# One substitution for all 128 diagonal blocks, a decay difference computed on ScalarE, and an earlier place for the first chunk's preparation, in a hybrid DeltaNet and sparse-attention layer

## The chip, the cores and the metric

One NeuronCore of one Trainium2 chip runs the whole program. The metric is device time in microseconds (us) of that core; the kernel before takes 1951.12 us, the median of three runs (1950.59 to 1951.98).

## The reference, cut to what matters

A decoder layer over 1024 positions of 1024 channels: two token mixers side by side (A, a gated DeltaNet; B, sparse attention), an output projection, a convolutional FFN and a gated embedding. The change lies in mixer A, which has 4 heads of 128 channels:

```
qkv = silu(causal_dwconv(concat(q, k, v), conv_w))          # 4 taps a channel
q, k = l2norm(q) * dk ** -0.5, l2norm(k)
beta = sigmoid(b);  g = -exp(a_log) * softplus(a + dt_bias)
# in chunk_gated_delta_rule, for each chunk and head:
gcum  = cumsum(g)
lower = beta[..., None] * (k @ k.T) * exp(gcum_i - gcum_j)  # strictly below the diagonal
sol   = triangular_solve(lower + I, [beta * exp(gcum) * k, beta * v])
...                                                         # then a scan over the chunks
o = rmsnorm(o, norm_w) * silu(z)
```

Everything is float32. The kernel works in chunks of 128 positions, which gives 8 chunks x 4 heads = 32 triangular matrices of 128 x 128.

## The kernel before, in words

**Projections.** A float32 product is three matmuls on halves of the operands (`mm3`, L345 to L347). The input `u` lies transposed in SBUF as `uh` and `ul`. Weights come in column tiles of 128: a DMA on SP's queue loads `raw`, ScalarE (ACT) makes the high half `whi` (L324), GpSimd (POOL) the low half `wlo` (L313). A tile over all 1024 positions is 48 matmuls `pj`. First come 12 convolution tiles in the order k (4), q (4), v (4), each in one of two PSUM areas in turn (`psJ[n % 2]`), so that tile n+2 must wait until tile n's area has been read. Reading it is a chain: ACT copies with the fourth tap's weight into `y` (L521), VectorE (DVE) adds three taps, each reading PSUM (L524), ACT applies Silu (L525). `norms` squares a finished k or q tile on ACT and sums it by a matmul with ones, `pss` (L507). Then come 4 z tiles (`gate_tile`, L562: ACT evacuates each half of a tile, `yz`, from one of two PSUM buffers, and a DMA, `gates_d`, stores it). Tiles are counted here from 0: 0 to 11 are the convolutions, 12 to 15 z, 16 onwards other gates, which fill the scan over chunks.

**What the scan needs first.** `gdn_small` (from L805) makes beta, the cumulated decay `gc`, the norm factors `rk`, and writes rows of them to DRAM. `gdn_inverse32` makes for each chunk c the matrix L: load two rows over all partitions (`row4`), scale k (L931), the decay difference on DVE (L899, 4 instructions) and its exponential on ACT (L904), `pkk` on TensorE (PE), two DVE products (L935, L936), and a round trip through DRAM (`ld`, L937 and L941) which lays the 32 x 32 diagonal blocks, 4 for each matrix, out as one block a partition: 128 partitions in all. There 31 steps of forward substitution, two DVE instructions each (L954 into `tmp`, L956 into `blk`), invert the blocks. This is done in two halves: chunks 0 to 3 on partitions 0 to 63, then chunks 4 to 7 on partitions 64 to 127. Each half ends with a DMA `xd` (L959), a transposing copy (L960) and a second DMA `xd` (L961); behind the second half a memset clears `blk` (L962).

**Preparing a chunk.** `gdn_prep(0)`, from L965, loads the inverted blocks and the blocks of L off the diagonal back (L978, 8 DMAs; L981, 3 DMAs) and multiplies them up to the inverse of the 128 x 128 matrix: `pz`, `pt`, `pt1n` and so on, ten groups of small matmuls.

**What sets the order.** Generators run by hand say what is issued behind what: the inverse is advanced once per convolution tile. A tile scheduler puts instructions into each engine's queue by its own model of time, within `tc.issue_after` limits; each engine then takes its queue in order, and waits where an operand is not there. The calls around the change are:

```
            if inv:
                next(inv, None)
            run_all(cv)
        run_all(inv)
        ...
        for n in range(4):
            run_all(gate_tile(n))
        NG = 8
        self.gdn_prep(0)
```

## Time and profile before

| what | value |
|---|---|
| median of the three runs | 1951.12 us |
| the profiled execution's own time | 1951.64 us |
| its span, first to last instruction | 1949.9 us |
| PE busy | 1839.1 us, 94% |
| DVE / ACT / POOL busy | 63% / 47% / 36% |
| mean granted TensorE clock | 0.977 of full speed |
| the stretch of the change | about 60 to 285 us of the span |

The page gives busy time by engine and by slice; the timeline lists each instruction with its start, its length and, in square brackets, how long the engine had been idle before it and what ended that. PE matmuls overlap in their modelled lengths; the spacing of their starts is what counts. A granted clock of 1.00 is TensorE's level of 2.4 GHz, 0.50 that of 1.2 GHz.

### The profile page before, as it was taken

The numbers are of one execution on the slowest core, as the hardware profiler recorded it, in microseconds if no ns is written. First come the engines' busy times: TensorE is split into PE (matmuls) and PEld (weight loads), VectorE is DVE, ScalarE is ACT, GpSimd is POOL, SyncE is SP. The second block draws the span as 40 slices with busy tenths as digits, with TensorE's granted clock in tenths as the row PEclk, the third lists the DMA queues.
The fourth block names the chain that finished last, engine by engine and source line by source line (L and its number), as shares of the span: only waits on it lengthen the run. The fifth ranks groups of instructions, "written<-read, shape, count | busy, mean of one in ns | idle before, by whom it ended". The sixth has DMA issues, their size and how long they took to land.

```text
span 1949.9 us, 25814 instructions
## 1 busy us (share of the span) xinstructions
PE 1839.1 (94%) x9247; PEld 1528.1 (78%) x9247; DVE 1224.2 (63%) x2347; ACT 920.3 (47%) x1816; POOL 711.6 (36%) x537
## 2 busy tenths in 40 slices
PE   7999989999999999999889949999999999999998
PEld 7888778888888887778778837787787877777786
DVE  4448934432277667766694587777677764868643
ACT  4344223323276667766663334444454544446432
POOL 2132212223122112321162166666666664555200
PEclk9999989999999999999999969999999999999999
DMA  5133333333311010200073212232323257246201
GB/s 166 33 95 103 101 83 93 97 87 95 100 28 34 28 39 28 71 23 23 22 248 121 97 55 81 92 103 88 122 83 103 92 184 259 72 146 208 88 33 43
DMA packets 182622, 178.67 MB, mean 92 GB/s; under 512 B 27549, under 2 KB 133342, under 8 KB 182494
## 3 DMA queue, kind: packets, MB, share of 16 engines
q1 hardware_dynamic: 180272, 170.33, 27.8%
q10 hardware_dynamic: 2222, 6.69, 0.9%
q8 instruction: 73, 1.20, 0.3%
q14 instruction: 55, 0.45, 0.1%
HBM read 132.65 MB, written 44.34 MB: 91 GB/s over the span
## 4 chain that ended last, share of the span: by engine, by line
PE 34%; DVE 5%; POOL 4%; issue 3%; ACT 2%; DMA 2%; SPq 0%; POOLq 0%; ACTq 0%; DVEq 0%
PE q L345 3%; PE q L347 3%; PE q L346 3%; PE n L345 2%; PE n L347 2%; PE n L346 2%; PE pg L347 2%; PE pg L346 2%; PE pg L345 2%; PE pwo L347 1%; PE pwo L345 1%; PE pwo L346 1%; POOL whl L313 1%; POOL wdhl L313 1%; DMA araw<-acts 1%
## 5 line engine op out<-in xcount | busy, mean ns | idle before, releaser
L345 PE MATMUL pj<-uh,whi 128*128 128x512 f32 x640 | 260.0, 407 | 6.0 <-DVE y L524 3.7
L347 PE MATMUL pj<-uh,wlo 128*128 128x512 f32 x640 | 255.2, 399 | 0.0
L346 PE MATMUL pj<-ul,whi 128*128 128x512 f32 x640 | 255.2, 399 | 0.0
L313 POOL TENSOR_TENSOR wlo<-raw,whi 128x1024 fp32r<-128x1024 f32 x48 | 117.3, 2446 | 310.5 <-ACT whi L324 266.6
L313 POOL TENSOR_TENSOR whl<-s,whl 128x512 fp32r<-128x512 f32 x88 | 131.3, 1500 | 57.2 <-ACT whl L1344 57.2
L345 PEld LDWEIGHTS pj<-uh,whi 128*128 128x128 f32 x640 | 121.5, 190 | 33.3 <-ACT yz L562 2.8
L347 PEld LDWEIGHTS pj<-uh,wlo 128*128 128x128 f32 x640 | 121.3, 190 | 29.0
L346 PEld LDWEIGHTS pj<-ul,whi 128*128 128x128 f32 x640 | 121.8, 190 | 25.8
L313 POOL TENSOR_TENSOR whl<-raw,whl 128x512 fp32r<-128x512 f32 x66 | 105.8, 1605 | 58.1 <-ACT whl L1344 55.5
L313 POOL TENSOR_TENSOR wdhl<-wd,wdhl 128x512 fp32r<-128x512 f32 x66 | 98.9, 1507 | 76.1 <-ACT wdhl L1344 74.8
L313 DVE TENSOR_TENSOR whl<-araw,whl 128x512 fp32r<-128x512 f32 x77 | 84.4, 1103 | 56.5 <-ACT whl L1344 54.0
L1226 ACT ACTIVATE Pt<-Pt,nm 128x640 f32<-128x640 f32 (+7 forms) x128 | 93.0, 729 | 36.6 <-DVE nm L1224 36.2
L345 PE MATMUL q<-mxh,whl 128*128 128x512 f32 x264 | 103.8, 396 | 4.1 <-ACT u L106 2.8
L1256 DVE TENSOR_TENSOR Tl<-pt,Th 128x512 fp32r<-128x512 f32 (+1 forms) x152 | 92.4, 616 | 22.1 <-ACT Th L1255 17.9
L346 PE MATMUL q<-mxl,whl 128*128 128x512 f32 x264 | 103.5, 392 | 0.0
L347 PE MATMUL q<-mxh,whl 128*128 128x512 f32 x264 | 102.9, 392 | 0.2 <-POOL whl L313 0.2
L1255 ACT ACTIVATE Th<-pt 128x512 fp32r<-128x512 f32 (+1 forms) x152 | 78.5, 538 | 43.7 <-PE po L1259 33.7
L324 ACT ACTIVATE whi<-raw 128x1024 fp32r<-128x1024 f32 x48 | 50.5, 1052 | 82.8 <-PE pj L346 54.1
L1252 PE MATMUL pt<-ident,Pt 128*128 128x128 f32 x528 | 84.6, 280 | 5.0 <-DVE Tl L1256 3.2
L1294 POOL TENSOR_TENSOR tm<-tm 128x128 f32<-128x128 f32 x32 | 14.7, 459 | 197.2 <-DVE tm L1292 157.4
L126 DVE SCALAR_TENSOR_TENSOR yg<-c,cv,yg 128x511 f32<-128x511 f32 (+1 forms) x88 | 82.0, 936 | 1.0 <-ACT yg L123 0.9
L1344 ACT ACTIVATE whl<-s 128x512 fp32r<-128x512 f32 x88 | 54.7, 624 | 55.8 <-PE n L347 44.1
(533 smaller groups left out, 5181.8 us busy)
## 6 DMA issues: line engine op xcount, KB each, us to landing
raw<-in_w_up SPq DMA_DIRECT2D x44, 512.0 KB
raw<-in_w_in SPq DMA_DIRECT2D x40, 512.0 KB
araw<-acts SPq DMA_DIRECT2D x35, 512.0 KB
acts<-sd SPq DMA_DIRECT2D x44, 256.0 KB
gates_d<-yz SPq DMA_DIRECT2D x40, 256.0 KB
acts<-yv SPq DMA_DIRECT2D x33, 256.0 KB
gt<-gates_d SPq DMA_DIRECT2D x32, 256.0 KB
wd<-in_w_down SPq DMA_DIRECT2D x7, 1024.0 KB
```

The costliest lines, as they stand in the source:

```text
L126: self.body.nc.vector.scalar_tensor_tensor(y, src, w, y, ALU.mult, ALU.add)
L313: return eng.tensor_sub(lo, src, hi.bitcast(F32)).ins
L324: nc.scalar.activation(hi, raw, AF.Copy)
L345: nc.tensor.matmul(ps, lh, rh, start=start, stop=False, skip_group_check=more)
L346: nc.tensor.matmul(ps, lh, rl, start=False, stop=False, skip_group_check=more)
L347: nc.tensor.matmul(ps, ll, rh, start=False, stop=stop, skip_group_check=more)
L1226: nc.scalar.activation(Pt[:, hh, 0:nk], Pt[:, hh, 0:nk], AF.Exp, scale=2.0 ** -(h0 + hh + 1), bias=nm[:, br, hh:hh + 1], accum_out=rs[:, b ...
L1252: nc.tensor.transpose(pt[:, b, hh], Pt[:, hh, (b0 + b) * P:(b0 + b + 1) * P], self.ident)
L1255: nc.scalar.activation(Th[:, 0:m], pt[:, 0:m], AF.Copy)
L1256: nc.vector.tensor_sub(Tl[:, 0:m], pt[:, 0:m], Th[:, 0:m].bitcast(F32))
L1294: nc.gpsimd.tensor_add(tm[:, 0], tm[:, 0], tm[:, 1])
L1344: self.nc.scalar.activation(hi, src, AF.Copy)
```

## The change

1. The substitution runs once over 128 partitions, after all 8 chunks, and is cut into four shares by `yield` (behind steps 8, 15 and 22). L is made by 4 fused DVE instructions of 128 x 128 in place of 2 of 128 x 512. Each `xd` DMA is 512 KB, and there are 2 in place of 4.
2. For L, the difference with the cumulated decay is 4 Relu activations on ACT with a bias (`ngc`, the negated `gc`) in place of 4 DVE instructions.
3. Each share of the inverse is issued behind the last DVE tap of the convolution tile (`issue_after`); `gdn_small` is split in two, and its first part stands behind tile 1's taps. `a_log` and `dt_bias` are loaded by two DMAs on ACT's queue at the start.
4. `gdn_prep(0)` is issued behind the last matmul of z's second tile (tile 13), not after all four.

```diff
+                if t == 1:
+                    for i, name in enumerate(("a_log", "dt_bias")):
+                        nc.scalar.dma_start(self.adb[:, i * H:i * H + H], rows_to_all(io[name], H))
...
             for j in (2, 1, 0):
                 d = 3 - j
-                nc.vector.scalar_tensor_tensor(y[:, d:], ps[:, 0:SEQ - d], cwt(j), y[:, d:], ALU.mult, ALU.add)
-            nc.scalar.activation(qkvT[i], y, AF.Silu)
-
+                last["DVE"] = nc.vector.scalar_tensor_tensor(y[:, d:], ps[:, 0:SEQ - d], cwt(j), y[:, d:], ALU.mult,
+                                                             ALU.add).ins
+            last["ACT"] = nc.scalar.activation(qkvT[i], y, AF.Silu).ins
+
...
         order = [4, 5, 6, 7, 0, 1, 2, 3, 8, 9, 10, 11]
-        inv = None
+        inv = small = None
         for n, i in enumerate(order):
             cv = conv(n, i)
             next(cv)
             if n and order[n - 1] < 8:
                 norms(order[n - 1])
+            run_all(cv)
+            with self.behind(*last.values()):
+                if n == 1:
+                    self.gp = self.g1 = self.pool(ges, "gdn")
+                    small = self.gdn_small(pss)
+                    next(small)
             if order[n - 1] == 7:
+                run_all(small)
                 inv = self.gdn_inverse32()
             if inv:
-                next(inv, None)
-            run_all(cv)
-        run_all(inv)
+                with tc.issue_after(last["DVE"]):
+                    next(inv, None)
+        with tc.issue_after(last["DVE"]):
+            run_all(inv)
...
         for n in range(4):
             run_all(gate_tile(n))
+            if n == 1:
+                with tc.issue_after(self.mm_last):
+                    self.gdn_prep(0)
         NG = 8
-        self.gdn_prep(0)
...
-        al = t32("al", H)
-        nc.sync.dma_start(al, rows_to_all(io["a_log"], H))
-        db = t32("db", H)
-        nc.sync.dma_start(db, rows_to_all(io["dt_bias"], H))
+        al, db = self.adb[:, 0:H], self.adb[:, H:2 * H]
...
         nc.vector.tensor_copy(gc, ps[:, 0, 0:n])
+        ngc = self.ngc = k32("ngc")
+        nc.vector.tensor_scalar(ngc, ps[:, 0, 0:n], -1.0, None, ALU.mult)
...
-        rk = self.rsqrt(kss, "rk")
+        yield
+        rk = self.rsqrt(kss[0][:, 0, 0:NC * H], "rk")
...
         E = self.g1.tile([P, H, P], F32, name="E", tag="E", bufs=1)
         for h in range(H):
-            nc.vector.tensor_scalar(E[:, h], gr[:, h], self.gc[:, c * H + h:c * H + h + 1], 0.0, ALU.subtract,
-                                    ALU.min if causal else ALU.max)
+            j = slice(c * H + h, c * H + h + 1)
+            if causal:
+                nc.vector.tensor_scalar(E[:, h], gr[:, h], self.gc[:, j], 0.0, ALU.subtract, ALU.min)
+            else:
+                nc.scalar.activation(E[:, h], gr[:, h], AF.Relu, bias=self.ngc[:, j])
...
-        for hf in range(2):
-            for c in range(hf * NC // 2, (hf + 1) * NC // 2):
...
-                E = self.decay(c, gr, False)
-                pk = self.mm4(self.psgt("pkk"), k, k)
-                L = self.g1.tile([P, H, P], F32, name="L", tag="Z", bufs=2)
-                nc.vector.tensor_mul(L, pk, E)
-                nc.vector.tensor_mul(L, L, self.bc(self.beta[:, c * H:(c + 1) * H]))
...
-            m_ = hn * 4
-            pp = slice(hf * m_, hf * m_ + m_)
-            X_ = X[pp]
...
-            for j in range(31):
-                m, w = 31 - j, j + 1
-                t = tmp[pp, 0:m * w].rearrange("p (a b) -> p a b", b=w)
-                nc.vector.tensor_mul(t, Ls[pp, j + 1:, j].unsqueeze(2).to_broadcast([m_, m, w]),
-                                     X_[:, j, 0:w].unsqueeze(1).to_broadcast([m_, m, w]))
-                nc.vector.tensor_sub(X_[:, j + 1:, 0:w], X_[:, j + 1:, 0:w], t)
-                if j in (12, 20):
-                    yield
-            nc.sync.dma_start(self.xd[0, pp], X_)
-            nc.vector.tensor_copy(Ls[pp], X_.rearrange("p i j -> p j i"))
-            nc.sync.dma_start(self.xd[1, pp], Ls[pp])
+        X, Ls = X[:], Ls[:]
+        for c in range(NC):
...
+            E = self.decay(c, gr, False)
+            pk = self.mm4(self.psgt("pkk"), k, k)
+            L = self.g1.tile([P, H, P], F32, name="L", tag="Z", bufs=2)
+            for h in range(H):
+                j = c * H + h
+                nc.vector.scalar_tensor_tensor(L[:, h], pk[:, h], self.beta[:, j:j + 1], E[:, h], ALU.mult, ALU.mult)
+            nc.sync.dma_start(self.ld[c], L)
...
+        nc.vector.memset(X, 0.0)
+        nc.vector.memset(X.rearrange("p i j -> p (i j)")[:, 0:1024:33], 1.0)
+        for j in range(31):
+            m, w = 31 - j, j + 1
+            t = tmp[:, 0:m * w].rearrange("p (a b) -> p a b", b=w)
+            nc.vector.tensor_mul(t, Ls[:, j + 1:, j].unsqueeze(2).to_broadcast([P, m, w]),
+                                 X[:, j, 0:w].unsqueeze(1).to_broadcast([P, m, w]))
+            nc.vector.tensor_sub(X[:, j + 1:, 0:w], X[:, j + 1:, 0:w], t)
+            if j in (8, 15, 22):
+                yield
+        nc.sync.dma_start(self.xd[0], X)
+        nc.vector.tensor_copy(Ls, X.rearrange("p i j -> p j i"))
+        nc.sync.dma_start(self.xd[1], Ls)
         nc.vector.memset(blk, 0.0)
```

Where the program order of the engines moves, in three places.

DVE, around the taps of the last convolution tile (tile 11: the rows with `y<-pj`), in the kernel before:

```order
L960 COPY blk<-blk 64x1024
L956 TENSOR_TENSOR blk<-blk,tmp 64x22x10
L524 SCALAR_TENSOR_TENSOR y<-pj,cvw,y 128x1023
L954 TENSOR_TENSOR tmp<-blk 64x231
L524 SCALAR_TENSOR_TENSOR y<-pj,cvw,y 128x1022
L956 TENSOR_TENSOR blk<-blk,tmp 64x21x11
L524 SCALAR_TENSOR_TENSOR y<-pj,cvw,y 128x1021
L954 TENSOR_TENSOR tmp<-blk 64x240
```

and in the changed one, where a step's second instruction is L972:

```order
L972 TENSOR_TENSOR blk<-blk,tmp 128x10x22
L970 TENSOR_TENSOR tmp<-blk 128x207
L525 SCALAR_TENSOR_TENSOR y<-pj,cvw,y 128x1023
L972 TENSOR_TENSOR blk<-blk,tmp 128x9x23
L525 SCALAR_TENSOR_TENSOR y<-pj,cvw,y 128x1022
L525 SCALAR_TENSOR_TENSOR y<-pj,cvw,y 128x1021
L970 TENSOR_TENSOR tmp<-blk 128x192
```

Before, tile 11's taps stand in the second half at step 11; behind them come 20 more steps of that half. Now they stand in the only substitution at step 22; behind them come 8 more steps. The taps of tiles 9 and 10 stand at steps 7 and 15.

PE, behind the last projection matmul of z (tile 15) in the kernel before, where every group of the first chunk's preparation stands:

```order
L347 MATMUL pj<-uh,wlo 128x512
L912 MATMUL pz_2025<-blk 128x128 x4
L912 MATMUL pt_2032<-Z,blk 128x128 x4
L992 MATMUL pt1n<-ident,TT 128x128 x4
L912 MATMUL pqk<-qT,kT 128x128 x4
L912 MATMUL pz_2068<-TT,blk 128x128 x4
L1010 MATMUL pkt<-ident,kT 128x128 x4
L1015 MATMUL pvt<-ident,vT 128x128 x4
L912 MATMUL pt_2088<-Z,T_2038 128x128 x4
L912 MATMUL pz_2152<-blk 128x128 x4
L912 MATMUL pu<-vT,T_2087 128x128 x4
```

and in the changed one, where the first group stands behind 37 of tile 14's 48 matmuls:

```order
L345 MATMUL pj<-uh,whi 128x512
L930 MATMUL pz_1853<-blk 128x128 x4
L346 MATMUL pj<-ul,whi 128x512
L347 MATMUL pj<-uh,wlo 128x512
L345 MATMUL pj<-uh,whi 128x512
L346 MATMUL pj<-ul,whi 128x512
L347 MATMUL pj<-uh,wlo 128x512
```

The others follow between matmuls of tile 15 (`pt_1860` behind 11 of them, `pt1n` to `pkt` behind 34, `pvt` behind 40), and the last three stand where they all stood.

SP's queue, from the stores of the inverted blocks to the loads of the preparation, in the kernel before:

```order
L959 DMA xd<-blk 64x1024
L320 DMA raw<-in_w_in 128x8x128
L961 DMA xd<-blk 64x1024
L563 DMA gates_d<-yz 128x512
L978 DMA blk<-xd 32x4x32 x5
L563 DMA gates_d<-yz 128x512
L978 DMA blk<-xd 32x4x32 x3
L981 DMA blk<-ld 32x4x32 x2
L981 DMA blk<-ld 64x4x64
```

and in the changed one:

```order
L975 DMA xd<-blk 128x1024
L575 DMA gates_d<-yz 128x512
L977 DMA xd<-blk 128x1024
L320 DMA raw<-in_w_in 128x8x128
L575 DMA gates_d<-yz 128x512
L994 DMA blk<-xd 32x4x32 x8
L575 DMA gates_d<-yz 128x512
L997 DMA blk<-ld 32x4x32 x2
L997 DMA blk<-ld 64x4x64
```

The chain of store, memset and load is as it was, but with stores of 512 KB; the `gates_d` in it are those of tiles 12 and 13 now, and were those of tiles 14 and 15.

## Rows read from the trace of the kernel before

**Rows 1.** The page: the engines' busy time, its share of the span, and their instructions.

```profile
PE 1839.1 (94%) x9247; PEld 1528.1 (78%) x9247; DVE 1224.2 (63%) x2347; ACT 920.3 (47%) x1816; POOL 711.6 (36%) x537
```

**Rows 2.** PE's waits from 0 to 700 us, the longest that is not at the start: the line that waited and what ended the wait; us in total, times, longest.

```profile
PE pz L912 <- DMA blk<-ld: 4.5, 1, 4.5
```

**Rows 3.** Timelines of PE and ACT around the first two convolution tiles: start, length, engine, line, what, and in brackets the idle time before and what ended it.

```profile
72.73 0.47 PE L345 MATMUL pj<-uh,whi 128*128 128x512 f32 x1 [1.95 <-DVE y L524]
66.23 0.21 ACT L853 ACTIVATE small<-small 128x4 f32<-128x4 f32 x1 [1.93 <-DMA small<-in_a_log]
```

**Rows 4.** Timelines of PE, DVE and ACT from 203 to 241 us: the waits of tile 11 and of tile 13's first half, the last of tile 11's taps, the Silu behind it on ACT, and the start of tile 14.

```profile
203.23 0.47 PE L345 MATMUL pj<-uh,whi 128*128 128x512 f32 x1 [1.79 <-DVE y L524]
230.75 1.28 DVE L524 SCALAR_TENSOR_TENSOR y<-pj,cvw,y 128x1021 f32<-128x1021 f32 x1
232.12 1.06 ACT L525 ACTIVATE vT<-y 128x1024 f32<-128x1024 f32 x1 [9.67 <-DVE y L524]
234.66 0.50 PE L345 MATMUL pj<-uh,whi 128*128 128x512 f32 x1 [1.64 <-ACT yz L562]
240.37 0.40 PE L345 MATMUL pj<-uh,whi 128*128 128x512 f32 x1
```

**Rows 5.** Busy time by stretch: the stretch and its length, then PE, PEld, DVE, ACT and POOL (instructions), then the granted clock, the DMA share and GB/s.

```profile
170.00:255.00 85.00, 81.56 (x367) 66.05 (x366) 77.20 (x161) 29.04 (x34) 23.23 (x9) 0.98 0.31 82
204.60:207.90 3.30, 3.30 (x10) 2.56 (x9) 2.79 (x5) 2.37 (x3) 1.80 (x1) 0.50 0.24 84
255.00:260.00 5.00, 5.00 (x23) 4.00 (x23) 1.30 (x1) 0.60 (x1) 0.36 (x1) 1.00 0.58 194
266.00:276.20 10.20, 7.29 (x31) 6.73 (x32) 1.00 (x2) 1.19 (x2) 0.26 (x1) 0.50 0.54 147
```

**Rows 6.** Timelines of DVE, SP's queue and PE from the end of the substitution to the first matmul of tile 16; among them one line of ACT, which waited for the store issued at 262.81 (256 KB from 128 partitions).

```profile
251.96 1.14 DVE L960 COPY blk<-blk 64x1024 f32<-64x1024 f32 x1
253.12 0.85 SPq L961 DMA_DIRECT2D xd<-blk  x1
258.70 1.76 DVE L962 MEMSET blk<- 128x2048 f32 x1 [5.61 <-DMA xd<-blk]
260.50 2.22 SPq L978 DMA_DIRECT2D blk<-xd  x5
262.81 0.38 SPq L563 DMA_DIRECT2D gates_d<-yz  x1
264.96 0.60 ACT L562 ACTIVATE yz<-pj 128x512 f32<-128x512 f32 x1 [1.12 <-DMA gates_d<-yz]
262.54 0.40 PE L347 MATMUL pj<-uh,wlo 128*128 128x512 f32 x1
267.44 2.05 PE L912 MATMUL pz<-blk 128*128 128x128 f32 x8 [4.51 <-DMA blk<-ld]
279.56 1.13 PE L912 MATMUL pz<-blk 128*128 128x128 f32 x8 [0.74 <-DMA blk<-xd]
281.39 0.48 PE L345 MATMUL pj<-uh,whi 128*128 128x512 f32 x1
```

**Rows 7.** DVE's groups by line, 160 to 255 us: times, busy us, mean ns, idle before.

```profile
L956 DVE TENSOR_TENSOR blk<-blk,tmp 64x31 f32<-64x31 f32 (+15 forms) x62 | 27.2, 439 | 1.8
L954 DVE TENSOR_TENSOR tmp<-blk 64x31 f32<-64x31 f32 (+15 forms) x62 | 25.1, 404 | 2.5 <-DMA blk<-ld 0.4 <-issue 0.3
L524 DVE SCALAR_TENSOR_TENSOR y<-pj,cvw,y 128x1023 f32<-128x1023 f32 (+2 forms) x15 | 19.1, 1274 | 2.9 <-ACT y L521 2.7
L899 DVE TENSOR_SCALAR E<-row,gc 128x128 f32<-128x128 f32 x20 | 4.3, 271 | 0.0
```

**Rows 8.** Timelines of DVE and POOL: a memset at 64 us, and substitution steps beside the making of a low half.

```profile
64.03 0.91 DVE L949 MEMSET blk<- 64x1024 f32 x1 [0.15 <-DVE sg L491]
...
233.84 0.42 DVE L954 TENSOR_TENSOR tmp<-blk 64x252 f32<-64x252 f32 x1
234.29 2.58 DVE L956 TENSOR_TENSOR blk<-blk,tmp 64x252 f32<-64x252 f32 x1
234.20 2.39 POOL L313 TENSOR_TENSOR wlo<-raw,whi 128x1024 fp32r<-128x1024 f32 x1 [14.19 <-ACT whi L324]
```

**Rows 9.** Timelines of PE, SP's queue and DVE: the last k k products and q's sums, chunk 7's L on its way through DRAM, and the step that waited for it.

```profile
175.63 1.58 PE L912 MATMUL pkk<-kT 128*128 128x128 f32 x12
200.35 0.34 SPq L937 DMA_DIRECT2D ld<-L  x1
205.92 2.79 DVE L954 TENSOR_TENSOR tmp<-blk 64x31 f32<-64x31 f32 x2 [0.41 <-DMA blk<-ld]
```

**Rows 10.** ACT's groups by line, 130 to 180 us and 280 to 420 us, and one of DVE's, 280 to 420 us.

```profile
L904 ACT ACTIVATE E<-E 128x512 f32<-128x512 f32 x5 | 3.2, 632 | 13.9 <-DVE E L899 13.9
L904 ACT ACT_TABLE_LOAD x3 | 3.8, 1283 | 0.1
L1069 ACT ACTIVATE jk<-o 128x128 bf16<-128x128 f32 x24 | 7.1, 298 | 45.1 <-DVE o L1063 45.1
L1041 DVE SCALAR_TENSOR_TENSOR r<-pw,bg,vT 128x128 f32<-128x128 f32 x24 | 6.8, 344 | 0.1
```

**Rows 11.** Timeline of DVE around the first L.

```profile
139.07 1.88 DVE L931 TENSOR_TENSOR kT<-kT,row 128x512 f32<-128x512 f32 x1 [0.88 <-DMA row<-rows_d]
141.96 0.68 DVE L935 TENSOR_TENSOR L<-pkk,E 128x512 f32<-128x512 f32 x1
```

More of the change, by code (lines that the diff above doesn't have):

```diff
@@ L346, in mm3 @@
         nc.tensor.matmul(ps, lh, rl, start=False, stop=False, skip_group_check=more)
-        nc.tensor.matmul(ps, ll, rh, start=False, stop=stop, skip_group_check=more)
+        self.mm_last = nc.tensor.matmul(ps, ll, rh, start=False, stop=stop, skip_group_check=more).ins
     def rstd_of(self, ss, n, scale, name):
@@ L442, in mixers @@
         self.cvw = keep.tile([P, 81], F32, name="cvw")
+        self.adb = keep.tile([P, 2 * H], F32, name="adb")
         ges = ExitStack()
@@ L507, in norms @@
                 nc.tensor.matmul(pss[0][:, 0, j:j + 1], sq[:, c * P:(c + 1) * P], self.ones, start=True, stop=True)
-            if i == 7:
-                self.gp = self.g1 = self.pool(ges, "gdn")
-                self.gdn_small(pss[0][:, 0, 0:NC * H])
             if i == 3:
@@ L523, in conv @@
                 d = 3 - j
-                nc.vector.scalar_tensor_tensor(y[:, d:], ps[:, 0:SEQ - d], cwt(j), y[:, d:], ALU.mult, ALU.add)
-            nc.scalar.activation(qkvT[i], y, AF.Silu)
+                last["DVE"] = nc.vector.scalar_tensor_tensor(y[:, d:], ps[:, 0:SEQ - d], cwt(j), y[:, d:], ALU.mult,
+                                                             ALU.add).ins
+            last["ACT"] = nc.scalar.activation(qkvT[i], y, AF.Silu).ins
+        last = {}
         order = [4, 5, 6, 7, 0, 1, 2, 3, 8, 9, 10, 11]
-        inv = None
+        inv = small = None
         for n, i in enumerate(order):
@@ L915, in gdn_inverse32 @@
     def gdn_inverse32(self):
-        nc, gp, n, hn = self.nc, self.gp, NC * H, NC * H // 2
+        nc, gp, n = self.nc, self.gp, NC * H
         self.ld = self.dr.tile([NC, P, H, P], F32, name="ld")
@@ L925, in gdn_inverse32 @@
         tmp = gp.tile([P, 256], F32, name="tmp", tag="T1")
-        for hf in range(2):
-            for c in range(hf * NC // 2, (hf + 1) * NC // 2):
-                rk = self.row4(1, c, "qk", 2)
-                gr = self.row4(0, c, "gr", 2)
-                k = self.chunk(1, c)
-                nc.vector.tensor_mul(k, k, rk)
-                E = self.decay(c, gr, False)
-                pk = self.mm4(self.psgt("pkk"), k, k)
-                L = self.g1.tile([P, H, P], F32, name="L", tag="Z", bufs=2)
-                nc.vector.tensor_mul(L, pk, E)
-                nc.vector.tensor_mul(L, L, self.bc(self.beta[:, c * H:(c + 1) * H]))
-                nc.sync.dma_start(self.ld[c], L)
-                for h in range(H):
-                    p0 = (c * H + h) * 4
-                    l = self.ld
-                    nc.sync.dma_start(Ls[p0:p0 + 4], bass.AP(
-                        tensor=l.tensor, offset=l.offset + (c * P * H + h) * P,
-                        ap=[[32 * H * P + 32, 4], [H * P, 32], [1, 32]]))
-                if c % 2:
-                    yield
-            m_ = hn * 4
-            pp = slice(hf * m_, hf * m_ + m_)
-            X_ = X[pp]
-            nc.vector.memset(X_, 0.0)
-            nc.vector.memset(X_.rearrange("p i j -> p (i j)")[:, 0:1024:33], 1.0)
-            for j in range(31):
-                m, w = 31 - j, j + 1
-                t = tmp[pp, 0:m * w].rearrange("p (a b) -> p a b", b=w)
-                nc.vector.tensor_mul(t, Ls[pp, j + 1:, j].unsqueeze(2).to_broadcast([m_, m, w]),
-                                     X_[:, j, 0:w].unsqueeze(1).to_broadcast([m_, m, w]))
-                nc.vector.tensor_sub(X_[:, j + 1:, 0:w], X_[:, j + 1:, 0:w], t)
-                if j in (12, 20):
-                    yield
-            nc.sync.dma_start(self.xd[0, pp], X_)
-            nc.vector.tensor_copy(Ls[pp], X_.rearrange("p i j -> p j i"))
-            nc.sync.dma_start(self.xd[1, pp], Ls[pp])
@@ new lines, in gdn_inverse32 @@
+        X, Ls = X[:], Ls[:]
+        for c in range(NC):
+            rk = self.row4(1, c, "qk", 2)
+            gr = self.row4(0, c, "gr", 2)
+            k = self.chunk(1, c)
+            nc.vector.tensor_mul(k, k, rk)
+            E = self.decay(c, gr, False)
[5 more added lines that the diff above has]
+            nc.sync.dma_start(self.ld[c], L)
+            for h in range(H):
+                p0 = (c * H + h) * 4
+                l = self.ld
+                nc.sync.dma_start(Ls[p0:p0 + 4], bass.AP(
+                    tensor=l.tensor, offset=l.offset + (c * P * H + h) * P,
+                    ap=[[32 * H * P + 32, 4], [H * P, 32], [1, 32]]))
+            if c % 2:
+                yield
@@ new lines, in gdn_inverse32 @@
+        nc.vector.memset(X, 0.0)
[7 more added lines that the diff above has]
+            if j in (8, 15, 22):
+                yield
```

## The prediction

> **What bounds the kernel now.** I read the page first. PE is busy for 94% of the span and no other engine for more than 63% [rows 1], so the time is PE's queue, and a change pays only by what PE waits for or by matmuls that run at the lower clock. Next come PE's waits in the first 700 us: the preparation of the first chunk waits 4.5 us for its loads, the longest of a few [rows 2]. The timelines give their places: tile 2 at 72.73 waits 1.95 us for taps on DVE [rows 3], tile 11 at 203.23 another 1.79, the first half of tile 13 at 234.66 1.64 for ACT [rows 4], and the preparation stands at 267.44 [rows 6]. The windows by stretch show what follows a wait: 3.3 us at a granted clock of 0.50 (the 1.2 GHz level) behind tile 11's wait, and 10.2 us behind the preparation's [rows 5]. At half the clock a stretch does half the work, so these cost 1.65 and 5.1 us on top of the waits. Last, DVE: between 170 and 255 us it is busy for 77.2 of 85 us [rows 5], 52.3 of that with 124 instructions of substitution [rows 7]. There DVE, not PE, sets when taps and inverse are done.
>
> **What goes.** *Tile 2.* ACT waited 1.93 us for `a_log` before it could copy tile 0, and DVE had work of `gdn_small` ahead of the taps. The changed order has both tiles' taps first, and the two loads are issued at the start, so PE's wait goes: 1.95 us [rows 3]. *Tile 11.* Its PSUM area comes free with tile 9's taps, which now stand at step 7 of the substitution. From its start, 186.6 (worked out below), sixteen instructions of at most 0.42 [rows 8] and 3.8 of taps end at 197; PE needs the area at 203.23 - 1.79 - 0.95 = 200.5. The 1.79 us [rows 4] and the 1.65 us of slow clock go: 3.4 us. *Tile 13.* Tile 11's taps ended at 232.0, its Silu followed at 232.12, and z's copies stood behind that on ACT; PE got its buffer 1.64 us late [rows 4]. With fewer DVE instructions ahead of those taps, 1.64 us go. *The end of z.* From the end of the last matmul of tile 15, 262.94, to tile 16's first at 281.39 are 18.45 us [rows 6]. The work in it at full clock is ten groups: the last two took 281.39 - 279.56 = 1.83 us, 0.92 each; seven such are 6.4 us, and three of half as many matmuls 1.4. That work stays, between matmuls of tiles 14 and 15. The rest, 18.45 - 7.8 = 10.6 us, is the wait of 4.5, the slow clock and three short waits for ACT and DVE, which now have projections to hide them. Together 1.95 + 3.4 + 1.64 + 10.6 = 17.6 us.
>
> **What comes: the first L.** Four chunks' k k products now stand three matmuls earlier in tile 7, and L of chunk 0 comes straight behind the scaling of chunk 3's k, which took 1.88 us where 0.69 is usual [rows 11]. The fourth product needs the buffer that this L frees. Between nothing (the row loads come earlier as well) and 1.2 + 0.7 = 1.9 us I take 1.0, the middle, for lack of a nearer row.
>
> **What comes: a new wait of the preparation.** The decisive question is when its first group, now behind 37 matmuls of tile 14, has its loads. Before, the last k k products ended at 177.2 [rows 9]; with 1.95 saved and 1.0 lost, 176.2. L of chunks 6 and 7 follow one behind the other, since E has one buffer. For one: four Relu at 0.30 us (a square of the same size, the nearest row), an exponential of 0.63, four fused DVE instructions at 0.34 [rows 10], 3.2 us; the first Relu overlaps, so 5 us for both, 181. The way through DRAM takes 205.92 - 200.35 = 5.6 us [rows 9]; the substitution starts at 186.6. Its length: a step over 128 partitions is not in the trace; it costs as much as one over 64, or up to twice that. A memset of 128 x 2048 took 1.76 us where one of 64 x 1024 took 0.91 [rows 6, 8]: the length along a partition counts, so I take the first (the other end, 22.6 us more, would go the way of case C below). Two halves took 52.3 us [rows 7]; in them are five stalls like the one at 234.29, 2.58 us where its neighbour took 0.42, beside a POOL instruction that began at 234.20 [rows 8]. Without 5 x 2.16 one half is 20.7 us; gaps of 0.03 us make it 22.6. Into it fall three sets of taps, 9 x 1.27 = 11.4 [rows 7], and the low halves of about four tiles, 8.6. It ends at 229.2, the copy (1.14) at 230.3. The stores: 5.6 us went from the second issue to the memset [rows 6]. The bytes in flight, two stores of 512 KB, one weight load and a gate store, are 1.84 MB, at 194 GB/s [rows 5] 9.5 us. I take the middle, 7.5. Memset 1.76, then 7.0 from its end to the first `pz` as before (260.46 to 267.44) [rows 6]: 246.6. PE would be there at 240.37 + 37 x 0.233 = 249.0 by the old times [rows 4], less 1.95 + 3.4 + 1.64 - 1.0 = 6.0: 243.0. So PE waits **3.6 us**, between 1.7 and 5.5 by the stores alone; one stall more or fewer moves it by 2.2, which makes 0 to 7. The clock after it: a wait of 1.79 us cost 1.65, one of 4.51 us cost 5.1 [rows 4 to 6]; between them, 3.9.
>
> By the Trainium skill ("SBUF — State Buffer", section "Door 1: The DMA port swizzle") a transfer's speed depends on how many of 16 ports its partitions reach, and 64 adjacent partitions reach no more than 32 do. By it the stores from 128 partitions would land in 5.6 us though they are twice as large, and the wait would be 1.7.
>
> **Costed at nothing.** The causal difference stays on DVE. SP's queue keeps its pattern, a weight load ahead of the preparation's loads and one behind them; weights are loaded a tile or more ahead of their matmuls, which hides the 7 us of loads in front of the second. Were it not hidden, tile 16 or 17 would wait, at most those 7 us. ACT's steps of the preparation now stand among z's copies; when `pz` is late, PE itself stands there, so the copies behind ACT's wait delay nobody else. The rest of the program moves as it is.
>
> **Sum.** 17.6 - 1.0 - 3.6 - 3.9 = 9.1 us against the profiled execution's 1951.64: 1942.5. That execution is 0.5 above the median of the runs, so I forecast 1942.0.
>
> **The rivals.** *A, no wait at all* (17%). If the stores land fast and one POOL stall fewer falls into the substitution, the loads are there when PE comes, and 16.6 us remain: 1951.64 - 16.6 - 0.5 = 1934.5. For it: 256 KB from 128 partitions were stored in 2.15 us (262.81 to 264.96) [rows 6]. Against it: a rate of 194 GB/s with all queues at work [rows 5]. The port rule named above points here, and this row agrees with it without proving it.
>
> *B, the wait only moves* (12%). The preparation waits 7 us, the clock costs 5.1, the first L 1.9, and tile 13 still waits its 1.64, since tile 11's taps stand among substitution steps that POOL stalls. 17.6 - 1.6 - 1.9 - 7 - 5.1 = 2.0: 1949.1, no change. For it: the same chain of store, memset and load stands in SP's queue; it did cost 4.5 us in front of PE, and nothing shortens it but an earlier start.
>
> *C, slower: the L chain on ACT* (7%). E has one buffer, so each chunk is a round trip ACT, DVE, ACT. One is 3.2 us against 1.1 (four of 0.27, rows 7), 0.63 and 0.68 before [rows 7, 10, 11], 2.4; eight make 6.4 us. If each also stands behind a Silu or a square of 1.1 us on ACT [rows 4], 8.8 more; two table loads of 1.28 [rows 10] more make 17.8. A start of the substitution later by x delays the preparation by x - 3.8 (a set of taps is then ahead of it), and PE has no other work to take. From x = 16 the wait passes 15 us, and with 5.1 for the clock the kernel is slower than before by over 0.2%; at 17.8 it is 1951.64 - 16.6 + 17.6 + 5.1 - 0.5 = 1957. Against it: only two chunks' L come late, and ACT is busy for 29 of 85 us [rows 5]. The Trainium skill ("ScalarE: Activation LUTs", section "Rules for kernel authors") says to put relu, max and min on VectorE, not on ScalarE. Here one costs 0.30 against 0.27 us; what counts is the queue in front of it.
>
> **How the numbers follow.** The forecast's own case has 64%: its waits of 1 to 7 us, the clock behind them and a first L of 0 to 1.9 give 1935.5 to 1947.5. The range runs from 1932.5, below case A, to 1949 and so leaves out C and half of B. A measurement of this kernel tells 0.2%, 3.9 us, from no change. Faster by more than that (under 1947.2): forecast and A, 81%. Within it: B, 12%. Slower: C, 7%.
>
> **What would show it.** Right: no wait of PE at tiles 2, 11 and 13; tile 16's first matmul straight behind tile 15 but for three groups; one wait of 1 to 5 us at `pz` in tile 14, ended by a load of `blk`, and a stretch at clock 0.50 behind it. The substitution starts near 187 and its copy ends near 230; a start past 195 speaks for C. Stores that land within 4 us speak for A. Wrong would be a new wait in tiles 7 to 11 for L or taps, or a difference that lies behind 285 us.

## The result, and the profile after

Four runs of the changed kernel had a median of 1934.88 us (1927.43 to 1935.95); the three runs of the kernel before, with a fourth, had 1951.55: the ratio is 0.9907, 95% interval [0.9891, 0.9922]. Two later series gave 1929.35 and 1929.30 us, ratios 0.9900 [0.9880, 0.9920] and 0.9901 [0.9886, 0.9916]. The forecast was 1942.0, in a range of 1932.5 to 1949: right in sign and inside the range, but the gain was 17 to 20 us where 9.1 were summed, and the two later medians lie under the range's 1932.5. The first number lies at rival A's 1934.5; its mechanism, no wait at all, is not what happened.

The page after, and of PE's waits from 0 to 700 us the four longest that lie between 60 and 300 us (they answer to [rows 2 to 4]):

```profile
PE 1837.5 (95%) x9247; PEld 1526.3 (79%) x9247; DVE 1194.3 (62%) x2267; ACT 934.1 (48%) x1851; POOL 710.1 (37%) x537
```

```profile
PE pkk L930 <- DVE L L955: 1.9, 1, 1.9
...
PE pz L930 <- DMA blk<-ld: 1.6, 1, 1.6
PE pgc L869 <- DVE small L867: 1.2, 1, 1.2
PE pj L345 <- DVE y L525: 1.1, 1, 1.1
```

PE's matmuls cost what they did: 1837.5 us busy against 1839.1 [rows 1]. DVE has 80 instructions and 30 us less. Where the waits stand, by the timelines of the same execution (PE, ACT, DVE and SP's queue; idle time before and its releaser in brackets):

```profile
65.80 1.06 ACT L324 ACTIVATE whi<-raw 128x1024 fp32r<-128x1024 f32 x1 [8.78 <-PE pj L346]
66.77 1.10 ACT L522 ACTIVATE y<-pj,cvw 128x1024 f32<-128x1024 f32 x1
71.96 0.47 PE L345 MATMUL pj<-uh,whi 128*128 128x512 f32 x1 [1.11 <-DVE y L525]
89.67 0.63 PE L869 MATMUL pgc<-small,triu 128*128 128x32 f32 x2 [1.17 <-DVE small L867]
146.84 1.35 PE L930 MATMUL pkk<-kT 128*128 128x128 f32 x8 [1.94 <-DVE L L955]
183.82 1.11 DVE L955 SCALAR_TENSOR_TENSOR L<-pkk,beta,E 128x128 f32<-128x128 f32 x4
192.06 0.21 DVE L970 TENSOR_TENSOR tmp<-blk 128x31 f32<-128x31 f32 x1 [2.70 <-DMA blk<-ld]
233.87 1.12 DVE L976 COPY blk<-blk 128x1024 f32<-128x1024 f32 x1
235.01 0.49 SPq L977 DMA_DIRECT2D xd<-blk  x1
239.57 1.76 DVE L978 MEMSET blk<- 128x2048 f32 x1 [4.59 <-DMA xd<-blk]
248.53 1.13 PE L930 MATMUL pz<-blk 128*128 128x128 f32 x8 [1.62 <-DMA blk<-ld]
270.01 0.48 PE L345 MATMUL pj<-uh,whi 128*128 128x512 f32 x1
```

The waits of tiles 11 and 13 [rows 4] are gone. Tile 16 begins at 270.01 where it began at 281.39 [rows 6], 11.4 us earlier; the span ends 17.6 earlier (1932.3 against 1949.9). The windows of this execution (columns as in [rows 5]) show two stretches at 0.50 (each is 6.8 us long by its exact ends), one of them in a place that the prediction has no term for, and the rate of all DMA queues together during the stores:

```profile
89.70:96.20 6.50, 6.50 (x17) 5.28 (x18) 3.88 (x6) 2.79 (x4) 0.00 (x0) 0.50 0.30 83
147.80:154.20 6.40, 6.40 (x25) 5.82 (x25) 4.37 (x7) 5.10 (x10) 0.00 (x0) 0.50 0.64 189
235.00:240.00 5.00, 5.00 (x24) 3.99 (x23) 0.43 (x1) 1.55 (x2) 0.73 (x1) 1.00 0.98 302
```

Behind the preparation's wait at 248.53 the clock stays at 1.00, unlike before.

**One measure for all runs below.** I split each profiled execution at tile 2's first matmul, at tile 16's, at the first transposes of the FFN (`pT_hn`, 1066.5 us before), at the FFN's 101st matmul `q` from `mxh` (1227.4 before) and at the end, and took from each stretch the *clock's cost*: half of every piece at granted clock 0.50, but for the one behind PE's last matmul. The rest is *net*: work and waits. Half is a little much: in the slow stretch at 90 us of the changed kernel the matmuls `pj` start 0.43 us apart, behind it 0.23, a factor of 1.83. All in us:

| kernel | median (ratio to before) | tile 16 begins | clock's cost to there | net to there | net, tile 2 to 16 | FFN's start, net | clock's cost in all |
|---|---|---|---|---|---|---|---|
| before | 1949 to 1952 | 281.4 | 11.9 | 269.4 | 196.7 | 145.6 | 42.7 |
| changed, first profile | 1934.9 (0.9907) | 270.0 | 6.8 | 263.2 | 191.2 | 144.1 | 37.5 |
| changed, second | 1929.4 (0.9900) | 265.0 | 1.7 | 263.3 | 191.4 | 144.4 | 29.0 |
| changed, third | 1929.3 (0.9901) | 267.1 | 3.4 | 263.7 | 191.7 | 144.0 | 30.7 |
| preparation late again | 1935.7 (0.9931) | 266.1 | 1.7 | 264.4 | 192.4 | 146.5 | 30.7 |
| decay on DVE again | 1931.5 (0.9911) | 267.5 | 6.8 | 260.7 | 189.1 | 144.0 | 35.8 |
| two halves again | 1950.1 (1.0001) | 282.7 | 13.7 | 269.0 | 196.6 | 146.4 | 44.4 |
| no ties | 1935.0 (0.9922) | 271.0 | 5.1 | 265.9 | 194.1 | 144.2 | 37.5 |
| single substitution alone | 1938.8 (0.9953) | 279.0 | 10.2 | 268.7 | 192.8 | 143.3 | 34.1 |
| small later | 1925.1 (0.9878) | 263.8 | 1.7 | 262.1 | 190.1 | 144.2 | 25.6 |
| small later, again | 1924.0 (0.9871) | 261.9 | 0.0 | 261.9 | 190.0 | 144.8 | 25.6 |
| ... and preparation behind tile 14 | 1925.8 (0.9875) | 262.7 | 1.7 | 261.0 | 189.0 | 144.0 | 29.0 |
| ... and copy first | 1928.6 (0.9887) | 261.5 | 0.0 | 261.5 | 190.2 | 144.2 | 27.3 |
| combined | 1932.9 (0.9916) | 267.3 | 3.4 | 263.9 | 192.2 | 143.2 | 35.8 |

The intervals of the ratios are 0.001 to 0.002 to either side.

The profiles are one execution each, and of the kernel before there is one alone. The mean granted clock that every run has on record gives the same split for the whole program: (1 - clock) x span is 39.7 us on average over 27 runs of the kernel before and 33.3 over twelve of the changed one. Of the 19.0 us between their mean spans some 6.4 are then the clock and 12.6 work and waits.

### The profile page after: what moved, and what is told of

Read it like the earlier page. It is cut to its first block, busy times and chain, and to the rows that moved or that the text cites. A ratio compares the mean times of both kernels' runs of the same rounds, so it can differ in the third digit from the quotient of the medians.

```text
span 1932.3 us, 25756 instructions
## 1 busy us (share of the span) xinstructions
PE 1837.5 (95%) x9247; PEld 1526.3 (79%) x9247; DVE 1194.3 (62%) x2267; ACT 934.1 (48%) x1851; POOL 710.1 (37%) x537
## 4 chain that ended last, share of the span: by engine, by line
PE 35%; DVE 7%; issue 3%; POOL 2%; DMA 2%; ACT 2%; POOLq 0%; DVEq 0%; SPq 0%; ACTq 0%
PE q L345 3%; PE q L347 3%; PE q L346 3%; PE n L345 2%; PE n L347 2%; PE n L346 2%; PE pg L347 2%; PE pg L346 2%; PE pg L345 2%; PE pwo L345 2%; PE pwo L346 2%; PE pwo L347 2%; DMA araw<-acts 1%; DVE whl L313 1%; PE dq L345 1%
## 5 line engine op out<-in xcount | busy, mean ns | idle before, releaser
L1360 ACT ACTIVATE whl<-s 128x512 fp32r<-128x512 f32 x88 | 54.7, 624 | 57.2 <-PE n L347 44.4
L126 DVE SCALAR_TENSOR_TENSOR yg<-c,cv,yg 128x1 f32<-128x1 f32 (+2 forms) x88 | 80.0, 914 | 0.9 <-ACT yg L123 0.9
```

The costliest lines, as they stand in the source:

```text
L126: self.body.nc.vector.scalar_tensor_tensor(y, src, w, y, ALU.mult, ALU.add)
L1360: self.nc.scalar.activation(hi, src, AF.Copy)
```

## The experiments

**The changed kernel twice more** (no edit).

> The changed kernel once more, unaltered. Stretches by the profile: start to tile 16's first matmul 281.39 us before and 270.01 changed; from there to the FFN's first transpose pT_hn 850.5 before and 849.5 changed; from there to the end 818 before and 813 changed. Theory (the last 5 to 6 us come from another instruction order in the FFN, which the scheduler chose): the three stretches come out as in the first profile, within 1 us each, and the times lie at 1934 to 1936. Rival (the FFN's length is scatter of the DMA traffic, as one run of 1927.4 among four suggests): the last stretch differs from 813 by 3 us or more, and the times spread over 1927 to 1940.

> The changed kernel a third time, beside the next three. In its first two profiles tile 16 began at 270.0 and at 265.0 us; the time that the half clock cost up to there (half of each stretch at 0.50) was 6.8 and 1.7 us, and without it both are 263.2 to 263.3. Theory (the waits are the same in every execution, and whether the clock falls behind one of them is not): tile 16 less the clock's cost is again within 0.5 us of 263.2. Rival (the loads and stores vary): it differs by 1 us or more.

The first of these: 265.0, 845.9 and 815.5 us for the three stretches (the second of them, as in that expectation, runs to the last group of `pT_hn`, at 1131.9 us before, and not to the first), so my theory that they repeat within 1 us is false, and the rival's 3 us in the last stretch did not come either. What differs is the clock. The same matmul `pgc` at the same time behind the same wait, in the second profile (timeline of PE, then the window around it):

```profile
89.67 0.41 PE L869 MATMUL pgc<-small,triu 128*128 128x32 f32 x2 [1.18 <-DVE small L867]
```

```profile
85.00:98.00 13.00, 11.82 (x61) 9.86 (x60) 7.96 (x19) 7.82 (x9) 2.35 (x1) 1.00 0.15 42
```

The clock stays at 1.00 here; in the first profile it was 0.50 for 6.8 us. The 1.94 us wait for the first L at 146.84 is absent too, and DVE's timeline shows why. In the first profile the second of two scalings of k begins 0.12 us behind a POOL subtraction and ends only behind it, in the second it begins ahead of it:

```profile
142.94 2.81 DVE L949 TENSOR_TENSOR kT<-kT,row 128x512 f32<-128x512 f32 x1
142.82 2.38 POOL L313 TENSOR_TENSOR wlo<-raw,whi 128x1024 fp32r<-128x1024 f32 x1 [10.54 <-ACT whi L324]
```

```profile
139.46 0.69 DVE L949 TENSOR_TENSOR kT<-kT,row 128x512 f32<-128x512 f32 x1
139.87 2.50 POOL L313 TENSOR_TENSOR wlo<-raw,whi 128x1024 fp32r<-128x1024 f32 x1 [10.66 <-ACT whi L324]
```

Net of the clock, tile 16 begins at 263.2, 263.3 and 263.7: the second expectation holds, if narrowly, once a stretch at half clock between 20 and 30 us (1.7 us, which the first two profiles do not have) is taken off as well. So the net length repeats within 0.5 us, though single waits come and go (the first L 1.94 or 0 us, tiles 11 and 12 none or 0.3 to 0.5 each, `pz` 1.6 to 2.3), and the clock behind a wait does not. The clock makes up most of the spread between the three profiles: 8.5 us of it against 2.6 net.

**The parts undone, one by one.** *Preparation behind all four z tiles again:*

```diff
         for n in range(4):
             run_all(gate_tile(n))
-            if n == 1:
-                with tc.issue_after(self.mm_last):
-                    self.gdn_prep(0)
+        self.gdn_prep(0)
```

> The changed kernel with the first chunk's preparation issued behind all four z tiles again. Theory 1 (moving the preparation is what saved the 10.6 us at the end of z): tile 16 starts some 10 us later than in the changed kernel, at 279 to 281, and the time is about 1944. Theory 2 (one substitution over 128 partitions saved it, since the loads are there at 248.5, before z ends at 262): no wait for loads is left, only the short waits between the groups, 2 us, and perhaps some slow clock; tile 16 at 271 to 274. The FFN's instruction order is the one of before in this kernel, so by the theory that this order costs 5 to 6 us the time is 1941 to 1944 in that case, and 1936 to 1938 if the order costs nothing.

Theory 2 has the mechanism and theory 1 is out, though tile 16 comes at 266.1, some 5 us ahead of theory 2's 271 to 274: net it is only 0.7 to 1.2 us later than in the changed kernel. No wait for loads is left; PE's waits there, by the view of waits from 60 to 300 us:

```profile
PE pt L928 <- ACT Z L999: 1.3, 1, 1.3
...
PE pt1n L1006 <- DVE TT L1002: 0.8, 1, 0.8
PE pu L928 <- DVE T L1032: 0.5, 1, 0.5
```

2.6 us of short waits are what the move removes, and it puts 1.6 to 2.3 of wait at `pz` in their place. The time of 1935.7 is 6.3 above the changed kernel beside it. Some 1 us of that is this stretch, and some 2 are the FFN's start, net 146.5 against 144.4 (see below); the rest is not placed.

*Two halves again*, with the fused L, the ties and the early loads kept (the scheduler puts the preparation behind z by itself):

```diff
-        for c in range(NC):
+        for hf in range(2):
+            for c in range(hf * NC // 2, (hf + 1) * NC // 2):
 ...
-        for j in range(31):
+            for j in range(31):
 ...
-                if j in (8, 15, 22):
+                if j in (12, 20):
```

> The changed kernel with the substitution in two halves of 64 partitions again, and nothing else undone; the scheduler then puts the preparation behind all z tiles by itself. Theory (the single substitution is what carries the first stretch): DVE has some 27 us more work, the loads come as late as before, PE waits 4 to 8 us for them, tile 16 at 279 to 284; the FFN's order is the one of before, so the time is 1948 to 1954. Rival (the taps tied ahead of the shares and the move are enough): tile 16 at 273 or earlier, time 1937 to 1943.

The theory: 1950.1, ratio 1.0001 [0.9991, 1.0012]. Tile 16 begins at 282.7. The wait is longer than the 4 to 8 us expected, since PE comes at 257.7, 5 us earlier than before. PE's timeline shows one wait that holds everything (the two shorter ones behind it are those of before):

```profile
268.74 2.05 PE L930 MATMUL pz<-blk 128*128 128x128 f32 x8 [11.03 <-DMA blk<-ld]
271.48 2.07 PE L930 MATMUL pt<-Z,blk 128*128 128x128 f32 x8 [0.69 <-ACT Z L1004]
274.33 1.12 PE L1011 MATMUL pt1n<-ident,TT 128*128 128x128 f32 x4 [0.78 <-DVE TT L1007]
```

Tiles 11 and 13 do not wait in this kernel; its second half ends with a copy at 254.8, where that of before stood at 251.96 [rows 6]. So these waits go with the other parts as well, but the time does not: without the single substitution, the fused L, the Relu, the ties and the early loads together give nothing. This kernel lost the early preparation too, and the FFN's order of the changed kernel. *Preparation late again*, from the same series, lacks the same two, so against it the substitution stands alone: 1935.7 and 1950.1, 14.4 us, of which net 4.6 lie ahead of tile 16. By the mean clocks of the runs half of the 14 us is the clock.

*The decay difference on DVE again* (`tensor_scalar` for both cases, no Relu):

> The changed kernel with the decay difference of L on DVE again (four instructions of 0.27 us in place of four Relu of 0.32 on ACT). Theory (the queue on ACT delays L: the substitution began at 192.1 where 186.6 was forecast): it begins 3 to 6 us earlier, the 1.6 us wait of the preparation goes, tile 16 at 267 to 269; time 1932 to 1934. Rival (DVE is the bound between 170 and 230, so work taken from it is what helps): tile 16 at 271 or later, time 1936 or more. The order behind tile 16 is that of the changed kernel, so only the first stretch should move.

Net the theory's 2 to 3 us are there: 260.7, and 0.6 us of wait at `pz`. Its start of the substitution, less 6.8 of clock, is 183.8 against 185.2 to 185.8, 1.5 to 2 us earlier, not 3 to 6. But in its profile a 0.58 us wait for L was followed by 10.2 us at half clock, and its times (1929.7 to 1932.9) are not under the changed kernel's on the same chip (1925.4 to 1931.4). In time this is inconclusive; net, Relu on ACT costs 2.5 to 3 us. The Trainium skill ("ScalarE: Activation LUTs", section "Rules for kernel authors") says to put relu on VectorE, for its speed per element. The trace agrees, with 1.28 us for four Relu and 0.87 for four `tensor_scalar`; here it counts because L's chain sets when the substitution begins.

*No ties of the shares behind the taps* (the two `issue_after(last["DVE"])` taken out):

> The changed kernel without the ties of the inverse's shares behind the taps; the scheduler keeps nearly the same order of taps and steps, but puts the preparation's first group 20 matmuls (4.7 us) earlier, behind 17 of tile 14's. Theory (the ties themselves are worth little; the loads come when they came): PE waits 4 to 7 us for them in place of 1.6 to 2.3, and a stretch at half clock follows, tile 2 to tile 16 less the half clock's cost 193 to 196, time 5 to 9 us above the changed kernel's 1929. Rival (without ties L and the substitution come earlier by as much): 191 to 192, time within 2 us of it.

The net length (194.1) and the time (1935.0, some 5.7 above 1929.3) are as expected, the place is not. PE's waits from 60 to 300 us:

```profile
PE pkk L928 <- DVE L L953: 2.9, 2, 1.5
PE pj L345 <- DVE y L525: 2.7, 3, 1.1
PE pz L928 <- DMA blk<-ld: 1.3, 1, 1.3
```

The preparation waits only 1.3 us; it is L and the taps that PE waits for, 2.9 and 2.7 (1.1 of the latter is tile 2's, as in the changed kernel).

**The single substitution alone**, put into the kernel before with the fused L and nothing else:

> The kernel before with the single substitution and the fused L alone: decay difference on DVE, no ties behind taps, gdn_small and the loads of a_log as before, preparation behind all z tiles. Theory (the single substitution carries most of the first stretch): tile 16 less the clock's cost comes down from 269.4 to 264 to 267, and the time is 1934 to 1942. Rival (without the ties the shares stand ahead of the taps, and PE waits at tiles 11 and 13 as before or longer): tile 16 less the clock's cost 267 or more, time 1943 to 1949.

The time, 1938.8, is in the theory's range: ratio 0.9953 [0.9938, 0.9968]. The net start of tile 16 is not: 268.7 is on the rival's side, but the rival's waits are not there. PE waits 6.1 us at tile 2 and 3.6 at the first L. From the view of waits, 60 to 300 us:

```profile
PE pj L345 <- DVE small L850: 6.1, 1, 6.1
PE pkk L912 <- DVE L L937: 3.6, 1, 3.6
PE pt L912 <- ACT Z L983: 1.5, 1, 1.5
```

No wait for loads and none for taps at tiles 11 and 13; from tile 2 to tile 16 it needs net 192.8 where the kernel before needs 196.7 and the changed one 191.2 to 191.7. So this part brings 4 of the 5 us in that stretch. Between ACT's copy of tile 0 and the last of its taps DVE does nine instructions of `gdn_small` here, two of them slow (2.36 and 1.77 us). The kernel before has the same calls, does four there and waits 1.95 at tile 2; so the 6.1 belongs to this kernel's instruction order, and no run shows what the changed places of the loads and of `gdn_small` are worth by themselves. Nor does a run have the single substitution without the fused L.

**Three edits on the changed kernel.** *`gdn_small`'s first part behind tile 2* (`if n == 2` in place of `if n == 1`), in two series:

> The changed kernel with the first part of gdn_small behind tile 2's last operations in place of tile 1's. Theory (its product with the triangle, pgc, stands in PE's queue three matmul steps into tile 3 and waits 1.2 us there for DVE, and the half clock behind that wait costs up to 3.4): the product then stands in tile 4, the wait is gone, and tile 16 less the clock's cost is 262 or a little under; no stretch at 0.50 near 90 us. Time 1 to 4 us under the unaltered changed kernel beside it. Rival (the wait moves to the rows that the first L needs): tile 16 less the clock's cost stays at 263 or rises, time the same.

> The kernel with the first part of gdn_small behind tile 2, unaltered, as the one that the next three stand beside. From tile 2's first matmul to tile 16's, less the half clock's cost, it took 190.1 us, and its time was 4.2 us under the changed kernel's. Theory (this gain is pgc's wait and what follows it, so it is in every execution): 189.6 to 190.6 again, and the time again 22 to 27 us under the kernel before. Rival (a lucky execution): over 191, time 18 to 21 us under the kernel before.

Both as the theory has it: `pgc` no longer waits, net 190.1 and 190.0, no stretch at 0.50 between 30 and 300 us in either profile. 1925.1 beside 1929.3, and 1924.0 in the next series: ratios 0.9878 [0.9858, 0.9898] and 0.9871 [0.9853, 0.9890]. Its medians are the lowest of all versions, under both kernels of the case; the next one's 1925.8 is not told from them. The 4.2 us against 1929.3 are net 1.6 in this stretch; most of the rest is the clock (25.6 us in all against 30.7).

*With that, the preparation behind tile 14*, and *a weight's high half on ACT behind the copy two tiles before*:

> The same with the first chunk's preparation issued behind tile 14's last matmul in place of tile 13's; its first group then stands ahead of tile 15, 11 matmuls (2.6 us) later. Theory (the 2.2 us that PE waits there are the only wait left, and they go): tile 2 to tile 16 less the half clock's cost at 188 to 189.5, the time 0 to 3 us under the kernel beside it. Rival (the groups that now stand together ahead of tile 16 wait for ACT and DVE instead, as they did with the preparation behind all z tiles): 189.6 to 191, the time within 1 us or above.

> The first of these four with the high half of tile n's weights issued on ACT behind the copy of tile n - 2; the decay difference stays on ACT. Theory (of the combined kernel's three edits this one made the new waits at tiles 9 to 12, 2.5 us, since a weight's high half now comes late): waits of 1 us or more at tiles 9 to 12, tile 2 to tile 16 less the half clock's cost 191.5 to 193, time 1 to 7 us above the first of these four. Rival (the decay difference on DVE made them): no such waits, 190 or less, tile 2 earlier by 0.8 us, time equal or under.

The first gains its 1.0 us net (189.0) and no time (1925.8 beside 1924.0, where 0 to 3 us under was expected): the wait at `pz` is gone, and `pu` ahead of tile 16 waits 1.5 us for DVE, as the rival has it. In the second tile 2 comes 0.6 us earlier (71.30, a wait of 0.35), and one wait of 1.32 at tile 12 takes the place, of the size that the theory has but a single one; net it is the same (190.2), against the theory. Its 4.6 us more in time are not in this stretch; the profile has them in the last (net 717.6 against 714.2, clock 6.8 against 1.7), and I cannot tell that from scatter.

*All three edits* (decay on DVE, small later, copy first):

> The changed kernel with three edits: decay difference of L on DVE again, the first part of gdn_small behind tile 2, and the high half of tile n's weights issued on ACT behind the copy of tile n - 2 (so tile 0's copy is not behind a weight). Theory (each removes a wait of 1 to 2 us of PE: the preparation's 1.6, pgc's 1.2, tile 2's 1.1): tile 16 less the clock's cost at 259.5 to 261.5, no or one stretch at half clock before it, time 3 to 6 us under the unaltered changed kernel beside it. Rival (first L's wait of 1.9 us takes up what comes earlier): tile 16 less the clock's cost 262.5 or more, time within 2 us.

Net 192.2, over the changed kernel: the rival's side, though not for its reason. The first L costs nothing; PE waits 2.6 us at `pz` and 2.5 at tiles 10 to 12, first for a weight's low half on POOL. Copy-first alone has 1.3 of these, the decay on DVE alone none, so neither edit by itself explains it; it stays open.

## Why the prediction was right, and where it was not

*Tiles 11 and 13:* right. Both waits and the slow stretch behind the first are gone; 0.3 to 0.5 us at each of tiles 11 and 12 come up in the second and third profile. (The wait at 234.66 before is at tile 13's second half, 24 matmuls ahead of tile 14; the rows and the prediction call it the first. The sum does not change.)

*Tile 2:* of 1.95 us 0.77 were saved. The row of `a_log` was read rightly, what is queued on ACT was not: tile 2's weight (65.80) stands ahead of tile 0's copy (66.77), which could start only when PE let go of a buffer; with the copy first, 0.35 us of the wait are left.

*A term that is missing:* `gdn_small` behind tile 1 puts `pgc` into tile 3, ahead of its operand: 1.17 us, and 3.4 of clock in the first profile (half of 6.8), none in the second and third. I had costed that move at nothing, and the order showed it.

*The first L:* 1.0 was forecast; 1.94 - 0.76 = 1.2 us in the first profile, no wait in the second and third. The cause named, a slow scaling of k, was the right one. What the prediction has no term for is the clock there. In the kernel before, the 0.76 us are followed by 10.2 us at 0.50, as long as behind the preparation's wait (the window has 10.0 of them):

```profile
142.70 1.75 PE L912 MATMUL pkk<-kT 128*128 128x128 f32 x8 [0.76 <-DVE L L935]
143.25:153.25 10.00, 10.00 (x36) 8.74 (x36) 7.75 (x17) 0.78 (x2) 0.00 (x0) 0.50 0.54 168
```

That is 5.1 of the 11.9 us of clock's cost ahead of tile 16. It came to 3.4 in the first profile and to nothing in the other two.

*The new wait:* 1.6 us (2.2 and 2.3 in the others) against 3.6. The substitution began at 192.1 in the first profile and at 185.4 and 187.5 in the others, where 186.6 was forecast. The first is late because PE was: the last k k products ended at 181.0, behind 6.8 us of clock's cost and the first L's wait, against 176.2 forecast and 172.5 and 174.3 in the others. From there L's chain took 4.0 to 5.6 us, with 4.8 forecast. The way through DRAM took 7.1 to 7.7 us in all three, not 5.6; that term was too small. The substitution's length was right (42.9 us to the copy's end against 43.7, with four steps of 2.3 to 2.7 us in it, as many as were summed). The stores landed in 4.6 us in all three, not 7.5; this is the term most in error. All queues together moved 302 GB/s then, where 194 was the rate with stores from 64 partitions [rows 5]. The port rule of the Trainium skill ("SBUF — State Buffer", section "Door 1: The DMA port swizzle") gave an estimate of 5.6 and was nearer than my middle of two rows. The runs agree with its main point, as much time for twice the bytes, though none changed the partitions alone: two stores from 64 partitions took 5.6 us before and 4.3 with two halves, two of twice the size from 128 took 3.8 to 5.4 over all kernels that have them. And PE came at 246.9 (239.7 and 241.8), not 243.0, for the waits and the clock above.

*The clock behind it:* 3.9 was forecast from two rows that both had a slow stretch. It was 0 in the first profile and 1.7 in the other two, and 0 behind 2.2 us in both profiles of *small later*. This is the step that fails most: I took the clock's fall for a function of the wait's length, and one wait of 1.17 us shows both. The trace of the kernel before could have said so: 0.76 us at the first L cost 5.1 us, and 1.95 at tile 2 and 1.64 at tile 13 cost none. The length of a wait is not all that differs: ahead of `pgc` and of the first L PE runs matmuls of one column (`pss`, 128x1), ahead of tiles 2 and 13 it does not. No run separates the two, and with the same matmuls ahead of it `pgc`'s wait had both outcomes.

*The end of z:* the 10.6 us went, but the change's fourth part is not why. With the preparation put back, the loads are there before z ends, and 2.6 us of short waits are left; the single substitution, and not the move, saved the rest.

*The sum to tile 16* was 9.1 and came to 11.4 (16.4 and 14.3 in the other profiles): net 5.7 to 6.2, the rest clock, 5.1 to 10.2. Ahead of tile 16 net gain and clock's gain are of one size, and I had the clock as an appendix to three waits. That the first series still fell inside the range is in part luck: the clock behind the first L and the FFN's order, gains both, are in no term of the sum.

*Behind tile 16* I said that the program moves as it is, and named a difference behind 285 us as what would prove me wrong. There is one. The change lets the scheduler choose another order at the start of the FFN. PE's waits at the FFN's start, 1066 to 1227 us, in the kernel before:

```profile
PE q L345 <- ACT whl L1344: 12.6, 1, 12.6
PE q L347 <- POOL whl L313: 5.9, 2, 5.7
...
PE n L345 <- DVE c L153: 1.5, 1, 1.5
PE n L345 <- ACT T3h L1344: 1.5, 1, 1.5
```

and over the same work in the changed one, first profile, 1054 to 1212 us:

```profile
PE q L345 <- ACT whl L1360: 13.0, 1, 13.0
PE n L345 <- ACT T3h L1360: 3.8, 1, 3.8
...
PE n L345 <- DVE c L153: 0.4, 1, 0.4
PE q L347 <- POOL whl L313: 0.3, 1, 0.3
```

A wait of 5.7 us for a weight's low half is gone, and one for `T3h` is 2.3 longer. Net, the FFN's start took 145.6, 146.4 and 146.5 us in the three kernels that have the order of before, and 143.2 to 144.8 in the eleven profiles with the changed order: about 2 us, by a split of all profiles and not by an edit made for it. The clock's cost there is 13.7 or 15.4 in either. Of the first profile's 17.6 us, 11.4 lie ahead of tile 16 and 3.1 here (160.9 to 157.8); the other 3 are spread over stretches whose net lengths differ by as much between profiles of one kernel, and one profile of the kernel before does not resolve them.

*The rivals.* A had the number by another way: no wait was wrong, the fast stores were right. B had its first L of 1.9 us in the first profile, but neither tile 13's wait nor 7 us at `pz` and the clock behind it. C's mechanism is there at a tenth of its size: without the Relu on ACT the substitution began net 1.5 to 2 us earlier, where C has 17.8. Most of the 5.5 us by which it came late in the first profile is the clock.

## What to carry to other kernels

A serial chain on one engine that runs over half the partitions twice is the first thing to fold: here it decided the stretch, and undoing it alone gave 14 of the 20 us back. Where a stage is priced from one profile, take the half-clock pieces out of both sides first, and compare what is left; the start of tile 16 repeated within 0.5 us here while the raw one differed by 5. And read in each engine's queue what stands ahead of the released instruction, for moved setup code too.

## What the runs showed of the hardware

The fall of TensorE's clock to its 1.2 GHz level behind a wait is not settled by the program: one wait of 1.17 to 1.18 us at the same place and time was followed by 6.8 us at 0.50 in one execution and by none in two others of the same kernel, and one of 1.62 us by none where 0.58 us in another kernel was followed by 10.2 us. In all, the clock's cost was 29.0 to 37.5 us in three executions of one kernel. A DVE step over 128 partitions takes as long as one over 64: 0.38 to 0.39 us for 220 elements a partition in both kernels' timelines. With two stores of 512 KB from 128 partitions under way the core's queues moved 302 GB/s over 5 us. A DVE instruction of 0.69 us took 2.8 when it began 0.12 us behind a POOL subtraction of 2.38 us, and 0.69 when it began ahead of one.
